# Half of the later modulation dot products on GpSimd and ScalarE, and a fourth raw buffer

## The chip, the cores and the metric

The kernel runs on one core of one Trainium2 chip. The metric is the device time of one execution in microseconds (us). Engines are written as in the profile: PE is TensorE, DVE is VectorE, ACT is ScalarE, POOL is GpSimd, SP is SyncE, which here issues the DMAs.

## The reference

A decoder trunk of two layers on 256 tokens with 2048 channels, all in float32. Layer 0 mixes tokens with multi-scale retention, layer 1 with a short gated convolution; each is followed by a SwiGLU feed-forward block of inner width 5632. What matters here is the conditioning: every sub-layer is shifted, scaled and gated by vectors that come from one vector c.

```python
c_act = jax.nn.silu(c)
for i in range(DEPTH):
    mod = (c_act @ w_mod[i] + b_mod[i])[:, None, :]
    sh1, sc1, g1, sh2, sc2, g2 = jnp.split(mod, 6, axis=-1)
    h = (rms_norm(x, norm1_g[i]) * (1.0 + sc1) + sh1).astype(x.dtype)
    ...                                    # retention (i = 0) or convolution (i = 1)
    x = (x + g1 * y).astype(x.dtype)
    h = (rms_norm(x, norm2_g[i]) * (1.0 + sc2) + sh2).astype(x.dtype)
    x = (x + g2 * swiglu(h, ffn_w_in[i], ffn_w_out[i])).astype(x.dtype)
return rms_norm(x, final_g).astype(x.dtype)
```

`w_mod` is 2 x 2048 x 12288, so `mod` is 2 x 12288 dot products of length 2048. That is 192 blocks of 128 outputs; a block is a 1 MB load, with the 128 outputs on the partitions and the 2048 products along the free axis.

## The kernel before

**Weights.** All projection weights lie in DRAM in the order of use, in 456 chunks of 128 x 2048 f32 (`w_all`). `fetch` loads a chunk into a buffer with the tag `raw`. `prepare` makes two pieces of 128 x 1024 from it: ACT copies a piece to float32r (`hi`, L402), DVE subtracts (`lo = raw - hi`, L405), and PE multiplies with both, which gives float32 accuracy from float32r passes. `hi` and `lo` have `PART_BUFS = 4` buffers each, so up to four pieces are alive: the one that PE reads, and three ahead of it. A `raw` buffer is free when both pieces of its chunk have been cast and subtracted.

**Matmuls.** `product` (L447, L450) takes, for each block of 128 x 128 weights, one matmul of 512 columns with `hi` and one of 256 columns with `lo`; a piece holds 8 blocks. `by_token` and `packed` (L460 to L462, L494 to L496) do the same with other shapes. PE's order is written out by hand. DVE, ACT and POOL are ordered by a list scheduler when the program is built, except in the opening stage (`RET_SPANS`), where the order of DVE and ACT is also by hand. Every engine then runs its list strictly in order. All loads go out from SP's queue, in order.

**Modulations.** The first 32 blocks (`SC1` and `SH1` of layer 0) are reduced in the opening stage at L755, from four `raw` buffers of a pool of their own, and are not touched. The other 160 come from `modulation(layer, which, j)`, which `paced` spreads over the first 71% of the weight blocks, by `plan_mod`, and `needed` calls at the latest before the column is used. A modulation loads its 1 MB block into a `raw` buffer (`mod_raw`, the same three buffers as the weights, `RAW_BUFS = 3`), and DVE multiplies it with `cb`, the activated c spread over all partitions, and sums along the row in one instruction (L318). POOL adds the bias and writes the column (L323, L325, L328). `high_priority(offset=MOD_PRIO)` makes the scheduler rank the sum behind other ready work.

**Root.** `roots_of` (L544, L546) makes the reciprocal root for a norm with a `pow` on POOL, in the same POOL queue as the modulation columns. `norm_spread` (L553) then needs it on PE, and `normed_outputs` (L992) needs it on DVE in each of the eight retention heads.

**Buffers in the opening.** While the first spans run, `prepare` fetches ahead until `RAW_BUFS - 1` chunks are loaded.

Of the kernel before, what the change touches and what calls it, by code (L numbers as in the profile page):

```python
# [13 lines left out]
AF = mybir.ActivationFunctionType  # L14
ALU = mybir.AluOpType
# [31 lines left out]
MOST = 0.045  # L47
MOD_PRIO = -300
STEPS = (8, 8, 20)
RAW_BUFS = 3  # L50
PART_BUFS = 4
LEFT, ENDS, EARLIER = 8, 2, 120

# [203 lines left out]
def trunk(ctx: ExitStack, tc: tile.TileContext, x_in, c_in, pos_in, w_mod, cols_in, gain_in, tab_in, w_all, out):  # L257
    nc = tc.nc
# [7 lines left out]
    def name(s):  # L266
        serial[0] += 1
        return f"{s}_{serial[0]}"

    def tmp(tag, shape=(P, S), dtype=F32, pool=work, bufs=None):  # L270
        return pool.tile(list(shape), dtype, tag=tag, name=name(tag), bufs=bufs)
# [6 lines left out]
    cb = const.tile([P, D], F32, tag="cb", name="cb")  # L278
# [28 lines left out]

    def mod_raw(t, pool=wpool, bufs=RAW_BUFS):
        raw = pool.tile([P, CHUNK], F32, tag="raw", name=name("raw"), bufs=bufs)
        nc.sync.dma_start(raw, w_mod[t])  # L310
        return raw

    def modulation(layer, which, j):
        t = layer * 6 * KT + which * KT + j
        raw = mod_raw(t)
        total = tmp("msum", (P, 1), bufs=4)
        with tc.high_priority(offset=MOD_PRIO):
            nc.vector.scalar_tensor_tensor(raw, raw, 1.0, cb, op0=ALU.mult, op1=ALU.mult, accum_out=total)  # L318
        b = b_mod[:, t : t + 1]
        norm = 0 if which < SH2 else 1  # L320
        if which in (SC1, SC2):
            m = tmp("mcol", (P, 1), bufs=4)
            nc.gpsimd.tensor_scalar(m, total, b, 1.0, op0=ALU.add, op1=ALU.add)  # L323
            dst = mod_a[layer][norm][:, j : j + 1]
            nc.gpsimd.tensor_tensor(dst, m, gain[norm][layer][:, j : j + 1], op=ALU.mult)  # L325
        else:
            dst = (mod_s if which in (SH1, SH2) else mod_g)[layer][norm][:, j : j + 1]
            nc.gpsimd.tensor_tensor(dst, total, b, op=ALU.add)  # L328
# [12 lines left out]
    def paced(n):  # L341

        units[0] += n
        due = 0
        for (a, i), (b, j) in zip(plan_mod, plan_mod[1:]):
            if units[0] >= a:
                due = min(j, i + (units[0] - a) * (j - i) // (b - a))
        allowed[0] = min(allowed[0] + n * MOST, 2.0) if n <= 64 else 0.0
        while todo and n_mod - len(todo) < due and allowed[0] >= 1.0:
            allowed[0] -= 1.0  # L350
            modulation(*todo.pop())

    def needed(layer, which, last=KT - 1):
        while any(m[:2] == (layer, which) and m[2] <= last for m in todo):
            modulation(*todo.pop())
# [14 lines left out]
    def fetch():  # L370
        raw = wpool.tile([P, CHUNK], F32, tag="raw", name=name("raw"), bufs=RAW_BUFS)
        nc.sync.dma_start(raw, w_all[n_fetched[0]])
        n_fetched[0] += 1
        fetched.append(raw)

    def prepare(between=None):
# [4 lines left out]
        if piece in (0, 2):  # L381
            if not fetched:
                fetch()
            raws[:] = [fetched.pop(0)]
            while first <= units[0] < early and len(fetched) < RAW_BUFS - 1 and n_fetched[0] < w_all.shape[0]:
                fetch()
# [697 lines left out]
    for i, g in enumerate(CONV_IN):  # L1084
        pending += [sums(g)] if i else normed(acc, 1, 0, g)
        while len(pending) >= 3:
            pb, pc, pu = pending[:3]
            pending = pending[3:]
            j = done
# [105 lines left out]
    total = mpool.tile([P, 2, 4], F32, tag="total", name="total")  # L1195
# [243 lines left out]
```

## Time and profile before

| | |
|---|---|
| median of 3 runs | 2592.86 us (2591.23 to 2596.55) |
| span of the profiled execution, first to last instruction | 2591.5 us |
| PE matmul busy | 2563.3 us (99%) |
| DVE busy | 2197.4 us (85%) |
| ACT busy | 1306.0 us (50%) |
| POOL busy | 125.9 us (5%) |
| DMA read | 685.08 MB, mean 266 GB/s |

The profiled execution has no time of its own beside its span; the span is 1.4 us below the median of the runs and inside their range. Busy times are sums over the span. Rows of groups give line, engine, operation, tiles, shape and count, then the busy time in us and the mean of one in ns, then the idle time of the engine just before them and what ended it. Line numbers are those of the kernel before.

### The profile page before, as it was taken

The page shows a single profiled execution, that of the slowest core. Times are in us where ns is not written, and L with a number is a line of the kernel's source. Part 1 is how long each engine was busy: PE and PEld are TensorE (multiplying, and loading weights), DVE is VectorE, ACT ScalarE, POOL GpSimd, SP SyncE. Part 2 cuts the span into 40 slices and gives each one's busy share as a digit, 9 for nine tenths or more (in the row PEclk, how much of TensorE's full clock was granted, in tenths as well). Part 3 has the DMA queues.
Part 4 walks back from the last instruction along what each step waited for, and adds up shares of the span by engine and source line. Part 5 has one row for each costly group of instructions (what it writes and reads, how often), then busy time and mean ns, then how long its engine had stood idle before and what let it go on. Part 6 is the DMA issues. An engine that isn't in the chain of part 4 may idle for free.

```text
span 2591.5 us, 36408 instructions
## 1 busy us (share of the span) xinstructions
PE 2563.3 (99%) x14181; PEld 2236.3 (86%) x14181; DVE 2197.4 (85%) x2762; ACT 1306.0 (50%) x1792; POOL 125.9 (5%) x232
## 2 busy tenths in 40 slices
PE   7999999999999999999999999999999999999998
PEld 6898889888889888888888898888998888888887
DVE  7988978787698887777778889988989998999978
ACT  5544543444456545334444454444565554556554
POOL 0000000110000000100001001000000000000001
PEclk9999999999999999999999999999999999999999
DMA  9975768767676888777877768877845565555654
GB/s 398 388 293 209 268 243 306 300 248 277 251 282 246 330 323 307 301 296 298 298 294 283 298 237 313 330 297 277 308 165 210 188 223 205 180 210 187 222 208 147
DMA packets 96688, 689.56 MB, mean 266 GB/s; under 512 B 10737, under 2 KB 12161, under 8 KB 13441
## 3 DMA queue, kind: packets, MB, share of 16 engines
q1 hardware_dynamic: 96514, 687.23, 71.3%
q8 instruction: 111, 1.82, 0.3%
q14 instruction: 63, 0.52, 0.1%
HBM read 685.08 MB, written 2.11 MB: 265 GB/s over the span
## 4 chain that ended last, share of the span: by engine, by line
PE 94%; DVE 3%; DMA 2%; issue 1%; ACT 1%; ACTq 0%; POOLq 0%; POOL 0%; DVEq 0%
PE bank L447 30%; PE bank L450 16%; PE bank L461 12%; PE bank L460 12%; PE bank L462 12%; PE bank L495 2%; PE bank L496 2%; PE bank L494 2%; PE bank L627 1%; PE bank L629 1%; PE bank L628 1%; DVE raw L755 1%; DMA raw<-w_all 1%; DVE lo L405 1%; PE bank L983 1%
## 5 line engine op out<-in xcount | busy, mean ns | idle before, releaser
L402 ACT CAST hi<-raw 128x1024 fp32r<-128x1024 f32 (+1 forms) x954 | 978.9, 1033 | 1015.8 <-PE bank L447 346.4
L405 DVE TENSOR_TENSOR lo<-raw,hi 128x1024 fp32r<-128x1024 f32 (+1 forms) x954 | 1133.9, 1197 | 322.6 <-ACT hi L402 317.3
L447 PE MATMUL bank<-h,hi 128*128 128x512 f32 x2016 | 699.3, 390 | 0.0
L450 PE MATMUL bank<-h,lo 128*128 128x256 f32 x2016 | 568.5, 282 | 0.0
L447 PEld LDWEIGHTS bank<-h,hi 128*128 128x128 f32 x2016 | 378.4, 188 | 79.2
L460 PE MATMUL bank<-hi,h 128*128 128x512 f32 x1032 | 405.0, 392 | 2.2 <-DVE rm L739 2.2
L461 PE MATMUL bank<-lo,h 128*128 128x512 f32 x1032 | 404.3, 392 | 0.0
L462 PE MATMUL bank<-hi,h 128*128 128x512 f32 x1032 | 402.7, 390 | 0.0
L450 PEld LDWEIGHTS bank<-h,lo 128*128 128x128 f32 x2016 | 381.0, 189 | 0.1
L318 DVE SCALAR_TENSOR_TENSOR raw<-raw,cb 128x2048 f32<-128x2048 f32 x160 | 365.5, 2284 | 15.7 <-DMA raw<-w_mod 15.3
L447 PE MATMUL bank<-mid,hi 128*128 128x512 f32 x922 | 319.8, 390 | 0.0
L450 PE MATMUL bank<-mid,lo 128*128 128x256 f32 x922 | 260.1, 282 | 0.4 <-DVE lo L405 0.4
L460 PEld LDWEIGHTS bank<-hi,h 128*128 128x128 f32 x1032 | 194.4, 188 | 40.7 <-DVE rm L739 2.8
L462 PEld LDWEIGHTS bank<-hi,h 128*128 128x128 f32 x1032 | 194.2, 188 | 40.8
L461 PEld LDWEIGHTS bank<-lo,h 128*128 128x128 f32 x1032 | 194.5, 188 | 40.4 <-DVE lo L405 3.3
L447 PEld LDWEIGHTS bank<-mid,hi 128*128 128x128 f32 x922 | 173.1, 188 | 36.2
L450 PEld LDWEIGHTS bank<-mid,lo 128*128 128x128 f32 x922 | 174.2, 189 | 0.7 <-DVE lo L405 0.7
L447 PE MATMUL bank<-rm,hi 128*128 128x512 f32 x496 | 172.5, 390 | 0.0
L496 PE MATMUL bank<-h,lo 128*128 128x256 f32 x512 | 146.4, 286 | 4.6 <-DVE lo L405 4.6
L494 PE MATMUL bank<-h,hi 128*128 128x256 f32 x512 | 146.1, 285 | 3.4 <-ACT h L783 3.4
L495 PE MATMUL bank<-h,hi 128*128 128x256 f32 x512 | 146.1, 285 | 0.7 <-DVE h L784 0.7
L450 PE MATMUL bank<-rm,lo 128*128 128x256 f32 x496 | 139.8, 282 | 0.0
(256 smaller groups left out, 3197.4 us busy)
## 6 DMA issues: line engine op xcount, KB each, us to landing
raw<-w_all SPq DMA_DIRECT2D x456, 1024.0 KB, 4.8
raw<-w_mod SPq DMA_DIRECT2D x192, 1024.0 KB, 5.2
x<-x_in SPq DMA_DIRECT2D x4, 512.0 KB, 5.3
out<-xt SPq DMA_DIRECT2D x4, 512.0 KB, 3.0
decay<-tab_in SPq DMA_DIRECT2D x8, 128.0 KB, 2.4
x<-gate_row SPq DMA_DIRECT2D x2, 512.0 KB, 4.8
last_gain<-gain_in SPq DMA_DIRECT2D x1, 1024.0 KB, 7.2
cols<-cols_in SPq DMA_DIRECT2D x1, 152.0 KB, 8.3
```

Of the source, the lines that this page charges most:

```text
L318: nc.vector.scalar_tensor_tensor(raw, raw, 1.0, cb, op0=ALU.mult, op1=ALU.mult, accum_out=total)
L402: nc.scalar.copy(hi, raw)
L405: nc.vector.tensor_tensor(lo, raw, hi.bitcast(F32), op=ALU.subtract)
L447: nc.tensor.matmul(pt, hi, h, start=fresh and k == g.ks[0], stop=False, skip_group_check=True)
L450: nc.tensor.matmul(pt[:, 1, :], lo, h[:, 0, :], start=False, stop=last and k == g.ks[-1], skip_group_check=True)
L460: nc.tensor.matmul(o, hi, w_hi, start=first, stop=False)
L461: nc.tensor.matmul(o, hi, w_lo, start=False, stop=False)
L462: nc.tensor.matmul(o, lo, w_hi, start=False, stop=last)
L494: nc.tensor.matmul(pt, hi, h[:, 0, :], start=first, stop=False, skip_group_check=True)
L495: nc.tensor.matmul(pt, hi, h[:, 1, :], start=False, stop=False, skip_group_check=True)
L496: nc.tensor.matmul(pt, lo, h[:, 0, :], start=False, stop=last, skip_group_check=True)
L627: nc.tensor.matmul(pt, hi, high, start=k == 0, stop=False, skip_group_check=True)
```

## The change

Every second modulation (odd `j`) is no longer one DVE instruction: POOL multiplies the block with `cb` in place, and ACT passes over the product with an identity activation whose accumulator gives the sum. The other half stays on DVE. The tag `raw` gets a fourth buffer of 8 KB per partition; room for it comes from the reserve for software-made DMA descriptors, set from 16 KB to 1 KB per partition. The kernel issues no DMA that would use it. `RAW_BUFS - 1` in `prepare` becomes 3 as well.

```diff
-RAW_BUFS = 3
+RAW_BUFS = 4
...
         with tc.high_priority(offset=MOD_PRIO):
-            nc.vector.scalar_tensor_tensor(raw, raw, 1.0, cb, op0=ALU.mult, op1=ALU.mult, accum_out=total)
+            if j % 2:
+                nc.gpsimd.tensor_tensor(raw, raw, cb, op=ALU.mult)
+                nc.scalar.activation(raw, raw, AF.Identity, accum_out=total)
+            else:
+                nc.vector.scalar_tensor_tensor(raw, raw, 1.0, cb, op0=ALU.mult, op1=ALU.mult, accum_out=total)
...
-    nc = bacc.Bacc("TRN2", target_bir_lowering=False, num_devices=1)
+    nc = bacc.Bacc("TRN2", target_bir_lowering=False, num_devices=1, dynamic_dma_scratch_size=1024)
```

In the built program 80 multiplies of 128 x 2048 stand on POOL, 80 sums on ACT and 80 of the 160 fused instructions are left on DVE. PE's order of work is the same, since it is written by hand; the lists of DVE, ACT and POOL are made anew.

## The prediction

> **What bounds the kernel now.** I read the page first, then PE's waits, then a table of windows.
>
> ```profile
> span 2591.5 us, 36408 instructions
> PE 2563.3 (99%) x14181; PEld 2236.3 (86%) x14181; DVE 2197.4 (85%) x2762; ACT 1306.0 (50%) x1792; POOL 125.9 (5%) x232
> PE   7999999999999999999999999999999999999998
> DVE  7988978787698887777778889988989998999978
> ```
>
> PE leaves 2591.5 - 2563.3 = 28.2 us of the span, at the two ends. A busy PE need not be a dense one, so I look at starts: in the timeline of PE the same matmul comes back after eight pairs of L447 and L450, with nothing between them.
>
> ```profile
> 1000.43 0.40 PE L447 MATMUL bank<-h,hi 128*128 128x512 f32 x1
> ...
> 1003.22 0.39 PE L447 MATMUL bank<-h,hi 128*128 128x512 f32 x1
> ```
>
> A piece of 1024 weight columns thus lasts 2.79 us on PE, 0.349 us a pair. The waits of PE (us in total, times, longest) are, over the whole span its largest, and from 200 to 1900 us, where all 160 modulations lie, the only two:
>
> ```profile
> PE bank L496 <- DVE lo L405: 4.6, 6, 1.1
> ...
> PE bank L983 <- DVE sp L512: 0.5, 1, 0.5
> PE bank L450 <- DVE lo L405: 0.4, 1, 0.4
> ```
>
> So in the stage that the edit works on, PE waits 0.9 us in 1700. Taking work off DVE can win no more than that there. The question is what the new order can lose.
>
> Windows of 100 us, the columns being PE, PEld, DVE, ACT and POOL busy, clock and DMA; below them the same windows for L318 alone (each modulation counts twice: the instruction and its accumulator read):
>
> ```profile
> 100.00:130.00 30.00, 27.83 (x169) 24.57 (x168) 28.32 (x31) 12.61 (x17) 0.00 (x0) 0.97 0.92 378
> 700.00:800.00 100.00, 100.00 (x649) 91.47 (x648) 88.83 (x136) 52.86 (x80) 4.69 (x10) 1.00 0.71 266
> 1000.00:1100.00 100.00, 100.00 (x579) 88.66 (x578) 78.85 (x88) 42.48 (x50) 11.70 (x18) 1.00 0.79 296
> 1600.00:1700.00 100.00, 100.00 (x578) 88.66 (x578) 90.07 (x123) 45.49 (x61) 5.14 (x13) 1.00 0.87 329
> 1800.00:1900.00 100.00, 99.58 (x661) 91.65 (x660) 91.43 (x136) 53.17 (x79) 3.31 (x10) 1.00 0.76 282
> ...
> 700.00:800.00 100.00, 18.32 (x16) 1.00 0.71 266
> 1000.00:1100.00 100.00, 22.94 (x20) 1.00 0.79 296
> 1600.00:1700.00 100.00, 28.36 (x26) 1.00 0.87 329
> 1800.00:1900.00 100.00, 18.33 (x16) 1.00 0.76 282
> ```
>
> **What the change removes.** The durations, from the groups and the DMA issues:
>
> ```profile
> L318 DVE SCALAR_TENSOR_TENSOR raw<-raw,cb 128x2048 f32<-128x2048 f32 x160 | 365.5, 2284 | 15.7 <-DMA raw<-w_mod 15.3
> L318 DVE DVE_READ_ACCUMULATOR raw<-raw,cb 128x1 f32 x160 | 13.1, 82 | 0.0
> L405 DVE TENSOR_TENSOR lo<-raw,hi 128x1024 fp32r<-128x1024 f32 x912 | 1107.2, 1221 | 315.9 <-ACT hi L402 310.8
> L402 ACT CAST hi<-raw 128x1024 fp32r<-128x1024 f32 x912 | 953.9, 1052 | 980.2 <-PE bank L447 346.4 <-PE bank L462 305.6 <-DMA raw<-w_all 179.9
> L986 ACT ACTIVATION_READ_ACCUMULATOR sq<-bank 128x1 f32 x16 | 3.1, 192 | 0.0
> raw<-w_mod SPq DMA_DIRECT2D x192, 1024.0 KB, 5.2
> ```
>
> DVE loses 80 x (2.284 + 0.082) = 189 us of work. None of it lies on the path, so the term is 0; what it gives is slack.
>
> **What it adds on POOL.** No row shows a long POOL operation. The nearest is DVE's own 2.28 us for the same two operands, the lower end. The upper end is twice that, 4.57 us, if POOL reads the operands one after the other through one port; I take it, because of the next rows. The Trainium skill (GPSIMD Engine Reference, section 3.1) gives 4497 ns for an elementwise add of this size on GpSimd against 2293 ns on VectorE, and advises VectorE for such work; by that price the sums below would be nearly the same.
>
> **POOL and DVE do not run freely beside each other.** The same POOL operation on 128x1, in the timeline, once beside an L405 (both operands in SBUF) and once beside an L506 (one operand in PSUM); its minimum, median and maximum in ns over 48; and a POOL operation while DVE ran two-operand work without a gap:
>
> ```profile
> 957.07 1.22 DVE L405 TENSOR_TENSOR lo<-raw,hi 128x1024 fp32r<-128x1024 f32 x1
> 957.25 1.19 POOL L323 TENSOR_SCALAR mcol<-msum,cols 128x1 f32<-128x1 f32 x1 [6.66 <-DVE raw L318]
> ...
> 972.24 0.29 POOL L323 TENSOR_SCALAR mcol<-msum,cols 128x1 f32<-128x1 f32 x1 [5.99 <-DVE raw L318]
> 972.25 0.42 DVE L506 TENSOR_TENSOR sum<-bank,low 128x256 f32<-128x256 f32 x1
> ...
> L323 POOL TENSOR_SCALAR mcol<-msum,cols x48: 288/401/3314, 426.4 to 1583.9; 128x1 f32<-128x1 f32 x48
> ...
> 2539.79 4.43 POOL L1220 TENSOR_TENSOR sums<-total 128x1 f32<-128x1 f32 x1 [659.15 <-ACT u L1370]
> ...
> L323 POOL TENSOR_SCALAR mcol<-msum,cols 128x1 f32<-128x1 f32 x48 | 39.3, 819 | 428.1 <-DVE raw L318 425.4 <-DVE rs L544 2.7
> ```
>
> Beside L405 POOL ended at 958.44, 0.15 us after the DVE operation (958.29); beside L506 it took 0.29. So POOL waits out a whole DVE instruction that reads two SBUF operands, 0.53 us on average (819 - 288 ns), up to 3.0 (3314 - 288) and more. What DVE does when POOL came first no row shows, because POOL never holds anything for long here. Its cost for DVE lies between 0 and the whole 4.57 us for each multiply; I take the whole, by the rows of the other direction. The Trainium skill (SBUF, State Buffer; section Who interferes with whom) says it of both directions: one shared port pair, an exclusive lock for the whole instruction, and the second one blocks. The trace agrees for POOL waiting on DVE.
>
> Each odd modulation then changes DVE's load by -2.37 + 4.57 = +2.20 us, 176 us in all. By windows: 1000 to 1100 has ten modulations, five odd: 78.85 + 11.0 = 89.9; 700 to 800 has four odd: 97.6; 1800 to 1900 has four: 100.2; 1600 to 1700 has 6.5: 104.4. The two above 100 cost PE what they exceed: 4.6 us.
>
> **What it adds on ACT.** The sum is at most two casts of half the length, 2.10, and the accumulator read, 0.19: 2.3 us, 184 us over 80, on an engine that is busy 50%. The price is the wait: ACT runs in order, and behind a sum whose multiply isn't done stand the `hi` casts. PE's cover against late pieces is three pieces ahead less the making of one: 3 x 2.79 - 1.05 - 1.22 = 6.1 us.
>
> In the built program I count, for each odd modulation, the casts d on ACT between the last cast from the `raw` buffer it takes over and its sum: 2 in six cases, 3 in twenty, 4 in 49, 5 in five. From the start of that last cast: buffer free at 1.05 + 1.22 = 2.3, block landed 5.2 later at 7.5, multiply done 0.53 + 4.57 later at 12.6, sum done at 14.9, the next cast and `lo` at 17.2. ACT comes to the sum at d x 2.79 + 1.05: 6.6, 9.4, 12.2, 15.0. PE needs the next piece at (d + 1) x 2.79 + 2.27 + 6.1: 16.7 for d = 2, so it is 0.5 late; 19.5 for d = 3, 2.3 to spare. With the lock the piece cast at 9.4 gets its `lo` at 13.8 and is needed at 16.7: 2.9 to spare. The cover isn't always full; casts wait for their block in this many cases from 200 to 1900 us:
>
> ```profile
> ACT hi L402 <- DMA raw<-w_all: 169.3, 80, 6.0
> ```
>
> That is 2.1 us each. So d = 2 costs 0.5 to 2.6, I take 1.5, six times: 9 us. d = 3 and 4 are covered; without 2.1 and with a POOL wait of 1 us more, d = 3 would lose 0.5 to 1, twenty times.
>
> **What is queued on POOL.** The `pow` of a norm (L546) stands behind a multiply and its column, which waits for the sum, in six of eleven places, the last two norms among them. Each can come later by 0 to 6.9 us (4.57 + 2.3), part of it covered; I take 1, so 6 us; at 4 it is 24.
>
> **The fourth buffer.** In the opening SP waited for a buffer (20 to 130 us):
>
> ```profile
> SPq L372 <- DVE lo L405: 59.5, 15, 8.6
> ```
>
> Loads go out earlier there, but DVE is busy 28.32 of 30 us. It can win at most PE's 4.6 us on `lo`, and can lose as much, since a chunk that goes earlier sends a modulation block later. I take a gain of 2 us. Later the buffer is the cover that keeps most d at 4.
>
> **Sum.** 9 + 4.6 + 6 - 2 = 17.6 us. The span lies 1.4 us under the median of the runs; added to the median 2592.9 it makes **2610 us**. This case's own range: 2598 to 2648, the top being 16 (d = 2 at 2.6) + 10 (d = 3) + 24 + 4.6.
>
> **Rivals.**
> *DVE is not held up* (not slower). If POOL's reads slip between DVE's, DVE sheds 189 us, the four windows above fall to 67 to 82 of 100 (each modulation moved takes 2.37 with it), and only the ACT order is left, which at full cover loses 6 x 0.5 = 3 us, against 2 won in the opening: 2594 us. For it: no row shows DVE waiting for POOL. Against it: the whole-instruction wait in the other direction. It decides if L405 beside a multiply stays near 1.22 us.
> *POOL is starved* (much slower). If multiplies get in only between trains of two-operand DVE work, as L1220 did after 4.43 us, the sum is late by 3 us more (the maximum of L323), d = 3 loses 1 to 2 and many of the 49 with d = 4 lose 1: 50 to 80 us, 2660. Against it: DVE idles 15% and L506 and its like let POOL in. It decides from a mean POOL wait of about 2 us. The granted clock adds to it: 0.97 from 100 to 130 us, where PE had waited, 1.00 in the other windows.
> *The opening decides* (faster). If the earlier loads remove PE's waits on `lo` and the rest stays covered: 4.6 us and 1 us of regained clock, 2587 us. Against it: DVE's load there doesn't change.
>
> **How the numbers follow.** Forecast 0.55, no hold-up 0.27, starved 0.12, opening 0.06. A comparison of this kernel tells about 0.2%, 5.2 us, from no change. Slower: 0.53 of the forecast and 0.12. Same: 0.02 of the forecast, 0.25 of the second, 0.01 of the last. Faster: the other 0.02 of the second and 0.05. Range 2588 to 2648; it leaves out most of the starved case and of the last.
>
> **What would show it.** Right: POOL rows of 4.5 us or more, some L405 stretched to 4 or 5 us, casts idle behind POOL, new PE waits on `lo` of 10 to 40 us in sum, chiefly at 200 to 750 and 1600 to 1900, none new at 1100 to 1400. Wrong: L405 unchanged in mean (1.22) with DVE near 2010 us; or multiplies that take 2.3 us; or PE waits that grow in 1100 to 1400, which would say that the cover of 6.1 us isn't there.

## The result and the profile after

The changed kernel takes 2741.39 us (median of four runs, 2735.12 to 2743.89), the kernel before 2592.27 us beside it. The ratio is 1.0569, with a 95% interval of 1.0554 to 1.0584: 149 us slower. The forecast was 2610 with a range of 2588 to 2648. The sign is right and the time is 131 us off; the added time is over eight times what was forecast (149 against 17.6 us).

In the changed kernel the lines of a step stand four further down: L402 is L406, L405 is L409, L447 is L451, L450 is L454. New are L319, POOL's multiply, and L320, ACT's sum; the fused DVE instruction is L322. The head of the page, for the profiled execution of 2735.12 us:

```profile
span 2733.1 us, 36520 instructions
PE 2611.3 (96%) x14181; PEld 2246.8 (82%) x14181; DVE 2229.8 (82%) x2602; ACT 1433.4 (52%) x1952; POOL 523.4 (19%) x312
PE   7999999999989999999999999999999999999998
DVE  7988977686698878667676779997789998899988
```

PE now leaves 2733.1 - 2611.3 = 121.8 us of the span, against 28.2. No slice stands out: the loss is spread thinly over the modulations. The windows of the prediction (PE, PEld, DVE, ACT, POOL, clock, DMA) say the same, and one more:

```profile
100.00:130.00 30.00, 28.85 (x182) 25.72 (x182) 29.20 (x33) 14.01 (x20) 0.00 (x0) 1.00 0.96 394
700.00:800.00 100.00, 95.46 (x526) 82.23 (x525) 76.75 (x97) 55.06 (x78) 22.97 (x14) 1.00 0.66 245
1000.00:1100.00 100.00, 92.95 (x507) 80.22 (x506) 80.81 (x75) 53.21 (x77) 38.51 (x26) 0.97 0.72 274
1100.00:1200.00 100.00, 96.93 (x553) 84.64 (x552) 62.41 (x71) 42.77 (x43) 31.47 (x20) 1.00 0.80 292
1800.00:1900.00 100.00, 94.77 (x526) 81.73 (x525) 79.78 (x96) 45.74 (x62) 30.82 (x14) 0.98 0.76 280
2100.00:2200.00 100.00, 100.00 (x449) 82.41 (x448) 92.86 (x110) 58.46 (x68) 0.00 (x0) 1.00 0.56 202
```

PE loses 3 to 7 of 100 us in these windows where modulations run (2 to 8 in all of them from 200 to 2000), also from 1100 to 1200, where DVE is busy only 62 of 100. After the last modulation (the last row) it loses nothing, with DVE at 93. So the loss doesn't follow DVE's load. The waits of PE, and then those of ACT (us in total, times, longest), point elsewhere:

```profile
PE bank L454 <- DVE lo L409: 46.2, 67, 2.4
PE bank L451 <- ACT hi L406: 25.1, 19, 5.4
```

```profile
ACT raw L320 <- POOL raw L319: 393.7, 73, 8.9
ACT hi L406 <- PE bank L466: 313.4, 294, 3.5
```

ACT stands behind POOL's multiply in 73 of 80 sums, 5.4 us each time. (The second row, casts that wait for PE, is that of the whole span: 42.7 of the 313.4 us lie between 200 and 2050 us.) The groups, shapes kept apart:

```profile
L409 DVE TENSOR_TENSOR lo<-raw,hi 128x1024 fp32r<-128x1024 f32 x912 | 1204.2, 1335 | 381.9 <-ACT hi L406 377.9
L319 POOL TENSOR_TENSOR raw<-raw,cb 128x2048 f32<-128x2048 f32 x80 | 390.9, 4887 | 438.7 <-DMA raw<-w_mod 285.1 <-DVE lo L409 46.9 <-issue 26.4
L320 ACT ACTIVATE raw<-raw 128x2048 f32<-128x2048 f32 x80 | 153.3, 1916 | 393.7 <-POOL raw L319 393.7
L1070 DVE TENSOR_TENSOR m<-sum,silu 128x256 f32<-128x256 f32 x44 | 39.6, 900 | 1.0
```

The multiply takes 4.89 us, and DVE is held as well: `lo` has a mean of 1335 ns instead of 1221, although DVE sits idle 378 us behind ACT's casts. A stretch of the timeline shows both at once (start, duration):

```profile
1388.35 2.36 DVE L409 TENSOR_TENSOR lo<-raw,hi 128x1024 fp32r<-128x1024 f32 x2 [1.42 <-ACT hi L406]
...
1390.82 4.62 POOL L319 TENSOR_TENSOR raw<-raw,cb 128x2048 f32<-128x2048 f32 x1 [8.42 <-DVE lo L409]
...
1391.08 4.65 DVE L1070 TENSOR_TENSOR m<-sum,silu 128x256 f32<-128x256 f32 x1
...
1395.47 1.92 ACT L320 ACTIVATE raw<-raw 128x2048 f32<-128x2048 f32 x1 [5.93 <-POOL raw L319]
...
1397.67 1.99 ACT L406 CAST hi<-raw 128x1024 fp32r<-128x1024 f32 x2
1399.57 0.36 ACT L508 COPY low<-bank 128x256 f32<-128x256 f32 x1
1401.48 0.42 ACT L1068 ACTIVATE silu<-sum 128x256 f32<-128x256 f32 x1 [1.55 <-DVE sum L510]
1401.80 1.99 ACT L406 CAST hi<-raw 128x1024 fp32r<-128x1024 f32 x2
...
1403.95 1.05 ACT L406 CAST hi<-raw 128x1024 fp32r<-128x1024 f32 x1
...
1407.07 1.05 ACT L406 CAST hi<-raw 128x1024 fp32r<-128x1024 f32 x1
...
1413.89 1.92 ACT L320 ACTIVATE raw<-raw 128x2048 f32<-128x2048 f32 x1 [5.51 <-POOL raw L319]
```

L1070 reads two operands in SBUF and has a mean of 0.42 us in the kernel before (L1066 there). Here it starts 0.26 us after the multiply and ends at 1395.73, 0.29 us after it (1395.44). ACT meanwhile idles 5.93 us ahead of its sum. Then it makes six casts in 10.5 us (1397.67 to 1408.12), in pairs back to back, and stands at the next sum, 5.51 us too early. Two suspects, then: the wait and the hold.

### The profile page after: what moved, and what is told of

The parts are those of the page before. It is cut to its first block, busy times and chain, and to the rows that moved or that the text cites. A ratio compares the mean times of both kernels' runs of the same rounds, so it can differ in the third digit from the quotient of the medians.

```text
span 2733.1 us, 36520 instructions
## 1 busy us (share of the span) xinstructions
PE 2611.3 (96%) x14181; PEld 2246.8 (82%) x14181; DVE 2229.8 (82%) x2602; ACT 1433.4 (52%) x1952; POOL 523.4 (19%) x312
## 4 chain that ended last, share of the span: by engine, by line
PE 46%; issue 16%; DVE 14%; DMA 10%; POOL 9%; ACT 5%; ACTq 0%; POOLq 0%; DVEq 0%; SPq 0%
PE bank L451 10%; DMA raw<-w_mod 10%; PE bank L465 8%; PE bank L466 8%; PE bank L464 8%; POOL raw L319 8%; DVE lo L409 7%; PE bank L454 6%; ACT hi L406 3%; DVE raw L322 2%; ACT raw L320 1%; PE bank L633 1%; PE bank L631 1%; PE bank L632 1%; DVE acc L526 1%
## 5 line engine op out<-in xcount | busy, mean ns | idle before, releaser
L409 DVE TENSOR_TENSOR lo<-raw,hi 128x1024 fp32r<-128x1024 f32 (+1 forms) x954 | 1230.8, 1306 | 388.0 <-ACT hi L406 383.9
L406 ACT CAST hi<-raw 128x1024 fp32r<-128x1024 f32 (+1 forms) x954 | 963.5, 1030 | 511.4 <-PE bank L466 290.7
L451 PE MATMUL bank<-h,hi 128*128 128x512 f32 x2016 | 713.4, 395 | 15.5 <-ACT hi L406 15.5
L454 PE MATMUL bank<-h,lo 128*128 128x256 f32 x2016 | 578.7, 287 | 32.3 <-DVE lo L409 31.6
L319 POOL TENSOR_TENSOR raw<-raw,cb 128x2048 f32<-128x2048 f32 x80 | 390.9, 4887 | 438.7 <-DMA raw<-w_mod 285.1
L451 PEld LDWEIGHTS bank<-h,hi 128*128 128x128 f32 x2016 | 383.1, 190 | 98.5 <-ACT hi L406 19.6
L454 PEld LDWEIGHTS bank<-h,lo 128*128 128x128 f32 x2016 | 385.2, 191 | 50.4 <-DVE lo L409 50.2
L320 ACT ACTIVATE raw<-raw 128x2048 f32<-128x2048 f32 x80 | 153.3, 1916 | 393.7 <-POOL raw L319 393.7
L451 PE MATMUL bank<-mid,hi 128*128 128x512 f32 x922 | 323.9, 393 | 9.6 <-ACT hi L406 9.6
L454 PE MATMUL bank<-mid,lo 128*128 128x256 f32 x922 | 262.9, 285 | 9.7 <-DVE lo L409 9.4
L451 PEld LDWEIGHTS bank<-mid,hi 128*128 128x128 f32 x922 | 174.2, 189 | 47.3 <-ACT hi L406 11.4
L322 DVE SCALAR_TENSOR_TENSOR raw<-raw,cb 128x2048 f32<-128x2048 f32 x80 | 182.9, 2286 | 24.3 <-DMA raw<-w_mod 23.8
L454 PEld LDWEIGHTS bank<-mid,lo 128*128 128x128 f32 x922 | 175.1, 190 | 16.2 <-DVE lo L409 15.8
L451 PE MATMUL bank<-rm,hi 128*128 128x512 f32 x496 | 173.0, 391 | 0.0
L500 PE MATMUL bank<-h,lo 128*128 128x256 f32 x512 | 148.0, 289 | 10.3 <-DVE lo L409 10.3
L498 PE MATMUL bank<-h,hi 128*128 128x256 f32 x512 | 146.9, 287 | 4.8 <-ACT h L787 3.2
```

Of the source, the lines that this page charges most:

```text
L319: nc.gpsimd.tensor_tensor(raw, raw, cb, op=ALU.mult)
L320: nc.scalar.activation(raw, raw, AF.Identity, accum_out=total)
L406: nc.scalar.copy(hi, raw)
L409: nc.vector.tensor_tensor(lo, raw, hi.bitcast(F32), op=ALU.subtract)
L451: nc.tensor.matmul(pt, hi, h, start=fresh and k == g.ks[0], stop=False, skip_group_check=True)
L454: nc.tensor.matmul(pt[:, 1, :], lo, h[:, 0, :], start=False, stop=last and k == g.ks[-1], skip_group_check=True)
```

## The experiments

In all of these runs the kernel before had medians of 2591.8 to 2593.12 us. The table has, for each, the time of POOL's work for one modulation, the time by which DVE is held for it, the idle time of ACT behind POOL over the whole run, and the result. DVE's hold is its busy time less that of the same list without POOL's work, 2035.8 us where half the sums are gone from DVE (`e4_act_no_pool`) and 2198.0 where none is (`e1_buf4_only`), divided by the multiplies; it is good to a few tenths, since busy times merge instructions that overlap. It counts what DVE lost, not how long POOL could have held it: a multiply beside an idle DVE holds nothing.

| kernel | POOL, us | DVE held, us | ACT idle, us | median us | ratio (95% interval) |
|---|---|---|---|---|---|
| the change | 4.89 | 2.4 | 394 | 2741.39 | 1.0569 (1.0554 to 1.0584) |
| e1_buf4_only | none | 0 | 0 | 2588.88 | 0.9986 (0.9977 to 0.9995) |
| e4_act_no_pool | none | 0 | 0 | 2588.76 | 0.9987 (0.9978 to 0.9996) |
| e2_split_buf3 | 4.97 | 2.2 | 363 | 2810.53 | 1.0843 (1.0827 to 1.0859) |
| e3_pool_beside | 3.77 | 2.6 | 0 | 2714.93 | 1.0476 (1.0458 to 1.0493) |
| e9_half_beside | 2.01 | 1.0 | 0 | 2606.09 | 1.0050 (1.0035 to 1.0065) |
| e11_hold_relieved | 3.62 | 2.5 | 0 | 2658.10 | 1.0252 (1.0237 to 1.0268) |
| e5_sum_first | 4.64 | 3.6 | 0 | 2748.26 | 1.0610 (1.0590 to 1.0630) |
| e6_late_sum | 4.95 | 3.2 | 92 | 2642.16 | 1.0197 (1.0180 to 1.0214) |
| e7_every_fourth (40) | 4.86 | 2.6 | 188 | 2629.70 | 1.0138 (1.0114 to 1.0163) |
| e8_quarters | 5.98 | 0.9 | 483 | 2809.00 | 1.0833 (1.0817 to 1.0849) |
| e15_late_quarters | 6.82 | 2.0 | 144 | 2637.38 | 1.0167 (1.0151 to 1.0182) |
| e16_three_quarters | 5.06 | 0.7 | 429 | 2739.93 | 1.0573 (1.0553 to 1.0593) |
| e10_memset | 1.81 | 0.0 | 28 | 2588.97 | 0.9987 (0.9977 to 0.9997) |
| e13_one_operand | 2.20 | 0.9 | 108 | 2589.09 | 0.9988 (0.9979 to 0.9997) |
| e12_two_memsets | 3.63 | 0.0 | 49 | 2589.48 | 0.9989 (0.9980 to 0.9998) |
| e14_long_memsets | 4.91 | 0.0 | 59 | 2589.99 | 0.9989 (0.9979 to 0.9998) |

### What costs nothing: the buffer and ACT's own work

`e1_buf4_only`, the fourth buffer alone, all sums on DVE:

```diff
-RAW_BUFS = 3
+RAW_BUFS = 4
...
+    nc = bacc.Bacc("TRN2", target_bir_lowering=False, num_devices=1, dynamic_dma_scratch_size=1024)
```

> Only the fourth raw buffer (and the smaller descriptor reserve); all 160 sums stay on DVE. Theory W (ScalarE stands behind the multiply, in order): the buffer is not the cause, 2588 to 2594 us. Theory L (DVE is held by GpSimd's multiply): the same. Theory S (the moved loads or the moved addresses cost): 2650 us or more.

It gains 2.9 us, 0.1%, with an interval that just leaves out no change. It is the only version here that beats both kernels with the whole computation.

`e4_act_no_pool`, the change less its multiply:

```diff
             if j % 2:
-                nc.gpsimd.tensor_tensor(raw, raw, cb, op=ALU.mult)
                 nc.scalar.activation(raw, raw, AF.Identity, accum_out=total)
```

> The changed kernel without GpSimd's multiply: ScalarE sums the raw block (the product with c is left out of every second modulation). Theory W: nothing to stand behind but the load, 2588 to 2605 us. Theory L: the same, since nothing holds DVE. Theory A (ScalarE's own 2.1 us per sum is too much for it): 2650 us or more.

2588.76: the 2.1 us of ACT for each sum are free, and DVE's 162 us of relief (2198.0 to 2035.8) buy nothing.

`e2_split_buf3`, the split with `RAW_BUFS = 3` and the old reserve:

> The split alone, with three raw buffers. The fourth buffer alone gained 3 us. If it is also cover for the wait behind POOL (a block is asked for earlier), the split without it costs more than the change: 2750 to 2790 us. If the wait goes only by the time from a buffer's release to the sum, the buffer gives back only its own 3 us: about 2744. Below 2735 would say that the buffer harms the split.

2810.53, 69 us more than the change. That is more than the 2750 to 2790 that was expected of a buffer that covers. The fourth buffer covers part of the split's cost; what it is worth alone (2.9) says little of that.

### The hold of DVE by itself

`e3_pool_beside`: all sums stay on DVE, three buffers; POOL multiplies into a buffer that nothing reads (the smaller reserve makes room for it).

```diff
             nc.vector.scalar_tensor_tensor(raw, raw, 1.0, cb, op0=ALU.mult, op1=ALU.mult, accum_out=total)
+            if j % 2:
+                idle = wpool.tile([P, CHUNK], F32, tag="idle", name=name("idle"), bufs=1)
+                nc.gpsimd.tensor_tensor(idle, cb, total.to_broadcast([P, CHUNK]), op=ALU.mult)
```

> All 160 sums on DVE as in the kernel before, three raw buffers; after every second sum GpSimd also multiplies two operands of 128x2048 into a buffer of its own that nobody reads. It holds DVE as the changed kernel does, and keeps ScalarE free of any wait for it. Theory L: the hold is the cost, and DVE is even fuller here, so 2700 to 2780 us. Theory W: the cover of about 6 us takes most of it, 2595 to 2630 us, with DVE stretched by some 200 us of busy time.

`e9_half_beside`, the same with 1024 columns:

> The kernel with an unread GpSimd multiply after every second sum on DVE, at half the length (128x1024): holds of about 1.8 us instead of 3.6. If the loss goes with the hold: half of 123 us, 2640 to 2665 us. If there is a cover that a hold has to exceed: 2595 to 2625 us.

`e11_hold_relieved`: ACT sums the block as loaded, DVE is relieved as in the change, and POOL then multiplies into an unread buffer:

```diff
             if j % 2:
-                nc.gpsimd.tensor_tensor(raw, raw, cb, op=ALU.mult)
                 nc.scalar.activation(raw, raw, AF.Identity, accum_out=total)
...
+            if j % 2:
+                idle = wpool.tile([P, CHUNK], mybir.dt.bfloat16, tag="idle", name=name("idle"), bufs=1)
+                nc.gpsimd.tensor_tensor(idle, cb, total.to_broadcast([P, CHUNK]), op=ALU.mult)
```

> The hold alone, with DVE relieved as in the change: ACT sums the block as loaded, with no wait for POOL, and after that POOL multiplies cb with the broadcast sum into a buffer that nothing reads (the product is left out). If the hold costs what is left over beside ACT's wait, 2620 to 2650 us, as with the late sum (2642). If the hold is the larger part, 2690 or more. If the DVE work that went away pays for the hold, 2588 to 2600. The difference to the kernel with the same idle multiply and all sums on DVE (2715) is what DVE's slack is worth.

Its page and its waits of PE:

```profile
PE 2582.2 (97%) x14181; PEld 2244.6 (84%) x14181; DVE 2238.3 (84%) x2602; ACT 1443.2 (54%) x1952; POOL 436.7 (16%) x312
```

```profile
PE bank L456 <- DVE lo L411: 42.4, 36, 2.6
```

A hold of 2.5 us, 80 times, costs 66 us with DVE relieved and four buffers, and one of 2.6 us costs 123 us with DVE full and three (`e3_pool_beside`). A hold of 1.0 us costs 13 us with DVE full (`e9_half_beside`). The hold is real and not linear. I read that as the cover taking in most of the short ones.

`e5_sum_first` swaps the two, ACT's sum ahead of POOL's multiply, so that the block is still held for both but ACT waits for the load alone (the sum is that of the block, the product is unread):

> The changed kernel with the two halves in the other order: ScalarE sums the raw block first, GpSimd multiplies it afterwards (the product is left out of the sum). All the work, the hold on DVE, the four buffers and the time a buffer is held stay; ScalarE no longer waits for GpSimd. Theory W: the loss goes, 2593 to 2625 us. Theory L: it stays, 2700 to 2745 us. Both half: 2650 to 2690 us.

2748.26, as slow as the change, with the largest hold (3.6 us). Taking ACT's wait on POOL away did not help here, since ACT now stands at its sum before the block has landed (141.6 us in 63 waits) and the multiply falls on a DVE that is busier. This run doesn't separate the two.

### The wait of ACT by itself

A memset only writes. `e10_memset` and `e12_two_memsets` put one or two in the multiply's place:

```diff
-                nc.gpsimd.tensor_tensor(raw, raw, cb, op=ALU.mult)
+                for _ in range(1):          # e12: range(2)
+                    nc.gpsimd.memset(raw, 1.0)
                 nc.scalar.activation(raw, raw, AF.Identity, accum_out=total)
```

> In place of the multiply POOL writes ones over the block in one memset (the product is left out); ACT's sum waits for it as before. A memset reads no operand. If POOL holds DVE only by operations with two SBUF operands, L409 stays near a mean of 1220 ns and DVE near 2040 us; what is left is ACT's wait, shorter by what the memset is shorter than 4.9 us. If ACT's wait is the larger part of the 149 us, and it is paid only beyond a cover of about 6 us, a memset of about 2 us leaves 2600 to 2640 us. If the loss were the hold of DVE alone, about 2590. If the hold comes with any POOL operation of this size, the mean of L409 rises to above 1270 and the time to above 2640.

> The same with two memsets one after the other, so that ACT waits about as long as behind the multiply, or half of it, without POOL reading anything (the product is left out). If ACT's wait makes 100 of the 149 us by itself, and the two memsets last together 4 to 5 us, 2670 to 2700 us; if they last only 2.5 to 3.5, 2610 to 2660. If the hold of DVE is the cause and the wait only goes with it, both memset kernels stay within 10 us of 2589.

Nothing lost, and DVE isn't held (2037.1 and 2034.6 us busy). The order of `e10_memset` is that of the change, 2 to 5 casts ahead of each sum. For two memsets the scheduler put the sums behind 3 to 6, which by itself takes wait away. `e13_one_operand` keeps the order and reads one operand:

```diff
-                nc.gpsimd.tensor_tensor(raw, raw, cb, op=ALU.mult)
+                nc.gpsimd.tensor_scalar(raw, raw, 1.0, 1.0, op0=ALU.mult, op1=ALU.mult)
```

> In place of the multiply POOL makes one operation that reads a single operand and writes it back, the block times 1 times 1 (the product with cb is left out). The order on every engine is that of the change: 2 to 5 casts ahead of ACT's sum. The memset of 1.81 us in this order lost nothing. If ACT's wait alone costs, this one loses by its length: with 3.5 us or less nothing (2589), with 4.5 to 5 us 2650 to 2690. If the wait costs only together with the hold on DVE, it stays within 10 us of 2589 at any length up to 5 us, unless the mean of L409 rises above 1270 ns. If POOL holds DVE with one operand too, that mean rises to 1300 or more, and the time comes out at 2650 or more.

It holds DVE 0.9 us and takes 2.20 us; nothing lost. `e14_long_memsets` is as long as the multiply, behind 4 to 7 casts:

```diff
-                nc.gpsimd.tensor_tensor(raw, raw, cb, op=ALU.mult)
+                for k in (CHUNK, CHUNK, 1408):
+                    nc.gpsimd.memset(raw[:, :k], 1.0)
```

> Three memsets on POOL, of 2048, 2048 and 1408 columns, which by the 1.81 us of one last as long together as the multiply, 4.9 us (the product is left out). POOL reads nothing, so DVE should not be held. The scheduler puts ACT's sum later for it: behind 4 to 7 casts, 5 in the middle, where the change has 4. If a wait of this length is harmless as long as DVE runs freely, 2587 to 2595. If waiting behind POOL for 4.9 us costs by itself, 2620 or more. With the late sum of the change, which took a similar place and cost 2642, the difference is then what the hold costs.

2589.99. By what was expected of these four runs, they would speak for the hold as the cause. But ACT's wait in them is short, 28 to 108 us over the 80 sums (0.3 to 1.3 us each) against 394: the multiply's place was taken by something shorter, or the sum stood later. None of them tests a wait as long as the change's. From the last one's timeline, two sums and the casts between them:

```profile
1309.16 1.92 ACT L321 ACTIVATE raw<-raw 128x2048 f32<-128x2048 f32 x1 [1.88 <-POOL raw L320]
...
1317.02 1.05 ACT L407 CAST hi<-raw 128x1024 fp32r<-128x1024 f32 x1 [0.58 <-PE bank L452]
1319.81 1.05 ACT L407 CAST hi<-raw 128x1024 fp32r<-128x1024 f32 x1 [1.74 <-PE bank L452]
...
1325.35 1.05 ACT L407 CAST hi<-raw 128x1024 fp32r<-128x1024 f32 x1 [1.51 <-PE bank L452]
...
1327.12 1.92 ACT L321 ACTIVATE raw<-raw 128x2048 f32<-128x2048 f32 x1 [0.45 <-POOL raw L320]
```

Here the casts wait for PE to give back a buffer, so the cover is full, and ACT comes 0.45 to 1.88 us early. So 4.9 us on POOL is no loss if the sum stands late enough and DVE runs free. Of these two conditions the next four runs tell which matters.

### The two told apart

`e8_quarters` cuts the multiply into four, so that DVE can get in between:

```diff
-                nc.gpsimd.tensor_tensor(raw, raw, cb, op=ALU.mult)
+                for i in range(0, CHUNK, DV):
+                    nc.gpsimd.tensor_tensor(raw[:, i : i + DV], raw[:, i : i + DV], cb[:, i : i + DV], op=ALU.mult)
```

> The changed kernel with GpSimd's multiply cut into four of 128x512; the work and ScalarE's wait for its end stay. If DVE gets in between the quarters, a hold is 1.2 us and the cover takes it: 2595 to 2650 us, with ScalarE's wait for GpSimd as long as before or longer. If GpSimd keeps the port through all four, or ScalarE's wait is what counts: 2715 to 2770 us.

The hold falls from 2.4 to 0.9 us, and the time rises to 2809.00, above all that was expected: the four take 5.98 us. `e16_three_quarters` brings that down to the change's length, with the pieces 512, 512, 512 and 128:

> The multiply over 512, 512, 512 and 128 columns (the last 384 are left as loaded), about 4.9 us in sum by the 1.53 us of a quarter, with the order of the change to within three of 80 sums and little hold on DVE (0.6 to 0.9 us for each). If a wait of the change's length in the change's order costs by itself, 2650 or more; with the 2590 of the long memsets behind more casts, the order is then the cause. If it costs only with the long hold on DVE, 2587 to 2620.

```profile
PE 2616.6 (96%) x14181; PEld 2255.6 (82%) x14181; DVE 2095.4 (77%) x2602; ACT 1434.1 (52%) x1952; POOL 533.5 (19%) x552
```

```profile
ACT raw L321 <- POOL raw L320: 429.0, 80, 9.9
```

2739.93, the change's time to 2 us, with DVE held for 0.7 us instead of 2.4, less than in `e13_one_operand`, where that was harmless. This is the sharpest run of the study: a wait of the change's length, in its order and with less than a third of its hold, makes the change's loss. The long hold adds little on top. POOL's work is 0.17 us longer here; between this run and `e8_quarters` 0.92 us more costs 69 us, so as an estimate 0.17 us is worth 13 us, and that much of the 149 may be the long hold. No run has a wait of this length in this order with nothing held at all.

`e6_late_sum` writes the change's sum 40 weight blocks later, so that the scheduler puts it behind 2 to 10 casts, mostly 4 to 8:

```diff
+LATE = 40
...
+        if j % 2:
+            late.append((units[0], lambda: summed_late(layer, which, j, t, raw, total), (layer, which, j)))
+            return
...
+        while late and units[0] >= late[0][0] + LATE:
+            late.pop(0)[1]()
```

> The changed kernel with ScalarE's sum written 40 weight blocks (about 14 us of TensorE) after its multiply, so that it seldom stands behind one that isn't done; the result is the same. Theory W (ScalarE stands behind GpSimd): 2600 to 2640 us. Theory L (the hold on DVE alone is enough): 2690 to 2745 us. If both must meet: 2640 to 2690 us.

`e15_late_quarters` does the same to the quarters:

> The multiply in four quarters, as in the kernel that lost 216 us, with the sum written 40 weight blocks later, as in the kernel that came to 2642. The quarters took 6.0 us in sum and held DVE 0.9 us for each multiply, about as much as the operation with one operand, which lost nothing. If ACT's wait in the wrong place made the 216 us, the late sum removes nearly all of it: 2590 to 2625 us. If the short holds of DVE made them, or if splitting a multiply costs in another way, 2700 or more stays.

Here the profile of the second, the same two lines:

```profile
PE 2579.2 (98%) x14181; PEld 2247.0 (85%) x14181; DVE 2197.2 (83%) x2602; ACT 1446.3 (55%) x1952; POOL 691.6 (26%) x552
```

```profile
ACT raw L318 <- POOL raw L328: 143.8, 37, 8.1
```

`e15_late_quarters` stayed above the 2625 us that were expected, so the place of the sum is most of it and not all. The late sum takes 99 us off the change and 172 off the quarters, although both hold DVE longer than without it (3.2 against 2.4, 2.0 against 0.9 us). Some 45 to 50 us stay. `e11_hold_relieved`, with the hold and no wait, lost 66, so the hold can explain them; that part of them comes from the waits left over (92 and 144 us) or from the later columns isn't excluded.

`e7_every_fourth` moves half as many (`j % 4 == 1`):

> Every fourth later modulation goes to GpSimd and ScalarE instead of every second: 40 multiplies, some 36 us apart. If each hold costs its own 1.8 us: half the loss, 2655 to 2675 us. If the loss comes from holds that follow each other before the pieces ahead have been made good: a quarter of it or less, 2595 to 2625 us.

37 us, a quarter of the loss for half of the multiplies. ACT waits as long behind each as in the change (188 us over 40, 4.7 us each); what differs is what a wait costs. With twice the distance the cover is partly refilled in between, as the casts that wait for PE show below.

## Why the prediction was wrong

The sign came from the right places, the lock and ACT's wait, and the prices of the single operations were near. Of the sum's terms only the 9 us for ACT's wait is of the kind that decided; the 4.6 us of DVE and the 6 us of the roots did not come about as such. The step that failed is the time at which ACT comes to its sum: it charged six of the 80 sums, and left the 20 with d = 3 and the 49 with d = 4 at nothing.

**The failed step: "ACT comes to the sum at d x 2.79 + 1.05".** It counts from the start of the last cast out of the buffer that the block takes over, puts casts at PE's pace, and has that buffer free after 2.3 us. So d = 4 comes at 12.2 us, when the multiply is as good as done (12.6). By this step the waits of ACT would be 6 x 6.0 + 20 x 3.2 + 49 x 0.4 = 120 us; the row says 393.7. I matched all 80 multiplies of the profiled execution with the program's order and took the time from the end of the instruction that frees the buffer to ACT standing at the sum. On this scale the step says 4.3 us for d = 2, 7.1 for d = 3, 9.9 for d = 4 and 12.7 for d = 5. The means are 6.6 us for d = 2, 5.9 for d = 3, 6.6 and 5.2 for d = 4 (after a weight chunk and after another modulation), 8.3 for d = 5: from 2 to 4 it doesn't grow with d. Over all it is 5.9 us, while the multiply is done at 0.04 + 5.77 + 4.89 = 10.7. Hence 4.9 us of idle each, on average.

Two things are wrong in the step. The first shows even where nothing is lost. In 38 of the 80 (33 of the 49 with d = 4, and all five with d = 5) the buffer is not freed behind a cast, but by DVE's fused sum of another modulation, so that the 2.3 us don't hold. `e10_memset` has the same order and lost nothing. Its trace, matched in the same way, has ACT at the sum 7.5 us after the release in these 38, where the step says 9.9 and 12.7; behind a `lo` it is 5.9, 7.1 and 8.8 us for d = 2, 3 and 4, nearer to the step's 4.3, 7.1 and 9.9. Over all 80 it is 7.5 us as well, so a multiply that is done at 10.7 would leave waits of 3.2 us. This is an estimate from two runs. The step's own mean is 1.5 us (120 over 80), and 4.9 was measured: about half of what it missed was there from the start.

The second is the pace. The 2.79 holds as long as casts wait for PE to return a buffer, as in the timeline of the long memsets. After a stall buffers are free, and casts come as fast as blocks and DVE allow: six in 10.5 us in the timeline above, 1.75 us each. So ACT comes to the next sum early and waits longer. A wait of 3.2 us and a sum of 1.92 + 0.18 make 5.3 us without a cast, inside the cover of 6.1 that the prediction worked out; with a wait of 4.9 it is 7.0, outside it, and in that stretch the next one comes 18 us later (1395.47 to 1413.89). The casts that wait for PE show how often the cover is full, in the kernel before (200 to 1900 us) and after (200 to 2050 us):

```profile
ACT hi L402 <- PE bank L447: 345.7, 246, 4.5
ACT hi L402 <- PE bank L462: 94.2, 61, 3.2
```

```profile
ACT hi L406 <- PE bank L451: 89.6, 66, 2.5
ACT hi L406 <- PE bank L466: 42.7, 32, 1.8
```

That is 440 us before and 132 after; between 35 of the 79 pairs of neighbouring sums no cast waits for PE at all. In `e7_every_fourth` the same two lines have 256 us (200 to 2000). So the traces show a state in which the cover is full (ACT idle 0.7 us each over the 80 in the long memsets, 59.3 in sum) and one in which it seldom refills; the prediction's single pass from a full cover couldn't see the second. How the first stall leads from one to the other was not followed. In front of this stands the order itself: the scheduler gives the sum the same place for a memset of 1.81 us and a multiply of 4.89. The prediction counted these places (2, 3, 4, 5) and did not ask whether they suit the length.

**The hold of DVE** was taken as the whole multiply, 4.57 us, and the timeline shows such whole holds, but the mean is 2.4: for 1.6 us of each multiply, in mean, DVE is idle (128 of 391 us in the trace). What made up the rest was not counted. The rule of the Trainium skill (SBUF — State Buffer, section Who interferes with whom) is that the lock blocks either side for a whole instruction; the trace agrees, as L1070 took 4.65 us beside the multiply. It agrees with the finer point as well, that GpSimd contends when it reads SBUF and not when it only writes: DVE is busy 2037.1 us with a memset, 2106.7 with a one-operand operation, 2035.8 with neither. The windows over 100 us of DVE that the sum charged with 4.6 us didn't come about (1600 to 1700 shows 90.27 and 1800 to 1900 shows 79.78), as everything runs slower and less work falls in a window.

**The multiply** was 4.57 by the prediction and 4.89 in mean. The Trainium skill's 4497 ns for an add of this size (GPSIMD Engine Reference, section 3.1) is close to the shortest one here, 4594 ns. **The sum on ACT** was 2.3 and is 2.1. **The landing and POOL's wait** were 5.73 together (5.2 + 0.53) and are 5.77.

**The pows on POOL** were charged with 6 us. PE waits for a root once, 1.8 us, before and after alike; the term is 0.

**The fourth buffer** was a gain of 2 us in the opening; alone it gains 2.9. That it is cover later is right and much larger than thought, 69 us, but not chiefly by keeping d at 4: without it ACT's wait behind POOL is no longer (363 against 394 us), while casts wait 247 us for their chunk to land (104 times) instead of 26.

**The rivals.** "POOL is starved" gave the best time, 2660, but by a mechanism that isn't there: the multiply is stretched by 0.3 us (4887 - 4594 ns) and starts when it was expected, not 2 or 3 us later. "DVE is not held up" is refuted by every run in which POOL reads two operands (0.7 to 3.6 us each). The prediction named what would show it wrong: PE waits that grow from 1100 to 1400. The window from 1100 to 1200 fell to 96.93.

## What to carry to other kernels

Before moving work to a slow engine whose result another engine waits for in order, find where the scheduler put the waiting instruction and how long it thinks the producer takes: a wait that is harmless behind enough other work can cost again and again in front of it. Count from what really frees the buffer, take the consumer's pace after a stall as well as that of an undisturbed pipeline, and compare wait plus operation with the cover; where the sum passes it, one stall can bring on the next. Two costs found by separate experiments (66 us for the hold, 147 for the wait with a small hold) needn't add: here their sum is 213 and the change lost 149.

## What the runs showed of the hardware beyond that

A multiply of 512 columns on POOL took 1.53 us in mean (5.98 us of busy time for four, 4.89 for one of 2048), so splitting lengthens it by a fifth; with the late sum on a busier DVE the four took 6.82. A POOL operation with a broadcast second operand took 3.62 to 3.77 us, one operand 2.20, a memset 1.81, for the same 2048 columns. The clock granted to PE fell with its stalls: 0.992 in mean after the change, 0.972 in `e2_split_buf3`, 0.998 or 0.999 in the kernels that lost nothing. As an estimate, 0.007 of 2733 us, 19 of the 149, is the slower clock and not the waits themselves.
